# Gate and up sums of a feed-forward as seven block products in place of eight

## The chip, the cores and the metric

The kernel runs on one NeuronCore of a Trainium2 chip. What counts is its time on the device in microseconds (us), the median of several executions. A profile is one more execution, recorded by the hardware: for every engine, which instruction ran when. The engines are TensorE (PE; its weight loads are shown as PEld), VectorE (DVE), ScalarE (ACT), GpSimd (POOL) and SyncE (SP), which here starts the transfers from memory. SBUF is the working memory of 128 partitions, PSUM the eight banks into which TensorE sums.

## What is computed

A trunk of two decoder layers on 512 tokens of 1024 features: the first layer mixes the tokens by a convolution module, the second by differential attention. Behind each follow a SwiGLU feed-forward of 2816 hidden features and a gated per-layer input. The change concerns the two feed-forwards:

```python
def rms_norm(x, g):
    y = xf * lax.rsqrt(jnp.mean(xf * xf, axis=-1, keepdims=True) + EPS)
    return (y * g.astype(jnp.float32)).astype(x.dtype)

def swiglu(x, w_gate, w_up, w_down):
    return (jax.nn.silu(x @ w_gate) * (x @ w_up)) @ w_down

u = rms_norm(h, ffn_norm_g[i])
h = h + swiglu(u, ffn_w_gate[i], ffn_w_up[i], ffn_w_down[i])
```

All arrays are float32.

## The kernel before

**Tiling.** Everything is held transposed: a chunk is 128 features (partitions) by 512 tokens. `h[0]` to `h[7]` is the state. A product needs more precision than one pass of TensorE gives on operands of type fp32r, so every operand is split in a high part (`hi`, a cast on ScalarE) and a low part (`lo`, the rest, a subtraction on VectorE), and `mm3` (L161 to L165) sums three passes: low weight by high input, high by high, high by low. `weight` (L144 to L159) loads 128 output features by up to 1024 inputs (512 KB) to a raw tile and splits it: the cast is L156, the subtraction L158. A tag such as `wraw` or `whi` names a set of buffers, and the second number its count: two `wraw`, four `whi`, four `wlo`. The tags `A`, `B`, `C`, `D` name buffers that the stages use in turn.

**The norm.** `Norm.split` (L213) multiplies a chunk of `h` by the norm's gain and splits it; the factor of each token, which needs the sum of squares over all chunks, comes later: `columns`, `diagonal` and `rows` make of it a row `rb` that is the same on all partitions (the copy is L255). The sums are made of the inputs without that factor, and `rb` is multiplied in at the eviction.

**The feed-forward** (`ffn`, L641 to L671) goes through the 22 hidden chunks in three parts of 8, 8 and 6. For each chunk it makes the gate sum and the up sum, eight input chunks by three passes each, and then evicts them: VectorE multiplies by `rb` (L657, L659), ScalarE applies Silu (L658), VectorE multiplies gate and up (L660), and the hidden chunk is split to the tile `B{i}` (L662, L663). At the end of a part `linear` (L609) makes the down sums: for each of eight output chunks m the products with the part's hidden chunks, added to `h[m]` by L667. The first two output chunks are made together, the others one by one. The sums take four PSUM banks (`mm`) in turn. In the second feed-forward the first operands come out of attention, else it is the same.

**The order of the work.** The program's text gives each instruction a place, but a planner that follows a model of the engines' times sets the order in which each engine's queue holds them: what is ready early may come ahead of what stands earlier in the text, and a tile is given a buffer of its tag when one is free. On the chip each engine then takes its queue in order, and waits where an instruction's inputs or its buffer are not ready. The transfers of weights are all issued from SP's queue.

**Lines the change touches.** `mm3` (L161), `Norm.split` (L213), the split behind the convolution (L600), `linear` (L609), `ffn` (L641), `stage_o` (L907) with the same tiles as `Norm.split`, and the order of the weights in memory (`_layout`, L1053).

Of the kernel before, what the change touches and what calls it, by code (L numbers as in the profile page):

```python
# [77 lines left out]
LT = 2  # L78
LA = 4
PACK = True  # L80
E1 = True
GLO = 1
QKV = (("q", 0, (0, 0, 0, 0)), ("v", 0, (1, 1, 1, 2)), ("q", 1, (1, 1, 1, 2)), ("q", 2, (1, 1, 2, 1)), ("v", 1, (1, 1, 2, 2)), ("q", 3, (1, 1, 1, 1)))
# [5 lines left out]
def trunk(ctx, tc, xT, pT, wts, diag, dww, vec, rel, onehot, lamv, out):  # L89
# [68 lines left out]
                eng.tensor_tensor(lo[:, cut], raw[:, cut], f(hi[:, cut]), ALU.subtract)  # L158
        return hi, lo  # L159

    def mm3(acc, a, b, first, last):  # L161
        (ah, al), (bh, bl) = a, b
        T.matmul(acc, al, bh, start=first, stop=False)  # L163
        T.matmul(acc, ah, bh, start=False, stop=False)  # L164
        return T.matmul(acc, ah, bl, start=False, stop=last)  # L165

    def weight_in_h(i, c):

# [37 lines left out]
    class Norm:  # L206
# [388 lines left out]
    with tc.manual_schedule(engines={V.engine, A.engine}):  # L595
        for c in range(NC + 2):
            if c < NC:
                V.tensor_tensor(y[c], y[c], lrow, ALU.mult)
                A.activation(y[c], y[c], AF.Silu, scale=col("ln_g", c), bias=col("ln_b", c))
                z.append((sb([P, S], f"A{2 * c}", 1, F32R), sb([P, S], f"A{2 * c + 1}", 1, F32R)))  # L600
# [8 lines left out]
    def linear(n_in, src, consume, group0=1, before=None, after=None, split={}, home=None, given={}):  # L609
# [31 lines left out]
    def ffn(norm, after):  # L641
        rb = None
        for at, (f0, n) in enumerate(PARTS):
            hid = []
            for i in range(n):
                wg, wu = weight(), weight()
                pg, pu = mm(), mm()
                for k in range(NC):
                    mm3(pg, wpart(wg, k), norm.u[k], k == 0, k == NC - 1)
                if rb is None:  # L650
                    norm.diagonal()
                for k in range(NC):
                    mm3(pu, wpart(wu, k), norm.u[k], k == 0, k == NC - 1)
                if rb is None:
                    rb = norm.rows()
                tg, tu = big(), big()
                V.tensor_tensor(tg, pg, rb, ALU.mult)  # L657
                A.activation(tg, tg, AF.Silu)  # L658
                V.tensor_tensor(tu, pu, rb, ALU.mult)  # L659
                V.tensor_tensor(tu, tu, tg, ALU.mult)  # L660
                hl = sb([P, 2, S], f"B{i}", 1, F32R)
                A.copy(hl[:, 0], tu)  # L662
                V.tensor_tensor(hl[:, 1], tu, f(hl[:, 0]), ALU.subtract)  # L663
                hid.append((hl[:, 0], hl[:, 1]))

            def add(m, acc):
                V.tensor_tensor(h[m], acc, h[m], ALU.add)  # L667
                if at == len(PARTS) - 1:
                    after.chunk(m)

            linear(n, hid, add, 2)  # L671

    def ple(norm, pp, after, last_cuts=1):
        def sums(m, cuts=1):
# [22 lines left out]
        for m in range(2, NC):  # L697
            for part in sums(m, last_cuts if m == NC - 1 else 1):
                gate(*part)

    n2 = Norm("ple_g0")
    ffn(norm, n2)
    norm = Norm("attn_g")
    ple(n2, pp, lambda m, cut: norm.chunk(m))

# [201 lines left out]
    def stage_o(hd):  # L907
        t = tp()
        for i in range(4):
            T.transpose(t[:, i * P : (i + 1) * P], osb[hd][:, i * P : (i + 1) * P], ident)  # L910
        hi = sb([P, S], f"A{2 * hd}", 1, F32R)
        lo = sb([P, S], f"A{2 * hd + 1}", 1, F32R)
        split_scaled(t, gains[:, 1:2], hi, lo)
        ot[hd] = (hi, lo)

# [99 lines left out]

    order = {m: last_block for m in (2, 3, 4, 5)}
    linear(NC, ot, add_attn, 2, heads_until, step, split=order, given={0: w_o0, 1: w_o1})
    n2 = Norm("ple_g1")
    ffn(norm, n2)

    def store(m, cut):
        nc.sync.dma_start(out[m][:, cut], h[m][:, cut])
# [30 lines left out]
def _layout(a):  # L1053
# [12 lines left out]
    def ffn(i):  # L1066
        g, u = _stationary(a["ffn_w_gate"][i]), _stationary(a["ffn_w_up"][i])
        r = []
        for f0, n in PARTS:
            for c in range(f0, f0 + n):  # L1070
                r += [g[c], u[c]]
            r += list(pad(_stationary(a["ffn_w_down"][i][f0 * P : (f0 + n) * P])))
        return r

# [77 lines left out]
```

## Time and profile before

| | |
|---|---|
| time, median of three runs | 1274.49 us (1273.96 to 1274.73) |
| profiled execution | span 1273.4 us, its only time on the page |
| instructions | 15438 |
| HBM read and written | 128.84 MB and 6.31 MB |
| granted TensorE clock, mean | 0.999 |

The span goes from the first to the last instruction. A row of a group shows line, engine, operation and tiles, then count, busy time and mean duration of one in ns, then the idle time of the engine just before them and what ended it. A row of the timeline begins with the start and the duration in us; the bracket is idle time before it with what ended it. Matmuls are pipelined: a row's 0.39 us is longer than the step from one start to the next. A row of a stretch shows its bounds, its length and the busy time of PE, PEld, DVE, ACT and POOL with their counts, then the granted clock, the share of the DMA engines and GB/s.

### The profile page before, as it was taken

The page shows a single profiled execution, that of the slowest core. Times are in us where ns is not written, and L with a number is a line of the kernel's source. Part 1 is how long each engine was busy: PE and PEld are TensorE (multiplying, and loading weights), DVE is VectorE, ACT ScalarE, POOL GpSimd, SP SyncE. Part 2 cuts the span into 40 slices and gives each one's busy share as a digit, 9 for nine tenths or more (in the row PEclk, how much of TensorE's full clock was granted, in tenths as well). Part 3 has the DMA queues.
Part 4 walks back from the last instruction along what each step waited for, and adds up shares of the span by engine and source line. Part 5 has one row for each costly group of instructions (what it writes and reads, how often), then busy time and mean ns, then how long its engine had stood idle before and what let it go on. Part 6 is the DMA issues. An engine that isn't in the chain of part 4 may idle for free.

```text
span 1273.4 us, 15438 instructions
## 1 busy us (share of the span) xinstructions
PE 1261.1 (99%) x5928; PEld 1046.3 (82%) x5928; DVE 714.3 (56%) x1042; ACT 523.5 (41%) x876; POOL 251.8 (20%) x227
## 2 busy tenths in 40 slices
PE   8999999999999999999999999999999999999998
PEld 7888788888888888888888888888888888888887
DVE  6997866543344334456776876655443444334545
ACT  5652554322233213244666877644221232123332
POOL 2763432000000000042436635131000000000120
PEclk9999999999999999999999999999999999999999
DMA  7565223223232222233432320242222222222231
GB/s 261 171 217 192 75 73 110 99 100 94 88 99 100 99 99 93 65 127 136 136 114 78 99 100 24 71 130 97 100 96 90 96 99 100 99 93 90 85 114 66
DMA packets 49141, 136.15 MB, mean 107 GB/s; under 512 B 5635, under 2 KB 10243, under 8 KB 49068
## 3 DMA queue, kind: packets, MB, share of 16 engines
q1 hardware_dynamic: 46944, 131.74, 30.9%
q10 hardware_dynamic: 2124, 3.43, 0.9%
q8 instruction: 46, 0.75, 0.2%
q14 instruction: 27, 0.22, 0.1%
HBM read 128.84 MB, written 6.31 MB: 106 GB/s over the span
## 4 chain that ended last, share of the span: by engine, by line
PE 90%; DVE 3%; DMA 1%; issue 0%; SPq 0%; ACT 0%; POOL 0%; DVEq 0%
PE mm L163 28%; PE mm L164 28%; PE mm L165 28%; PE mm L880 1%; DVE sc L447 1%; PE sc L848 1%; PE sc L847 1%; PE tp L867 1%; PE sc L396 1%; PE mm L396 1%; PE tp L801 1%; PE mm L352 1%; PE tp L196 0%; DVE wlo L158 0%; DVE big L522 0%
## 5 line engine op out<-in xcount | busy, mean ns | idle before, releaser
L156 ACT CAST whi<-wraw 128x1024 fp32r<-128x1024 f32 (+2 forms) x209 | 213.1, 1026 | 555.5 <-PE mm L165 365.3
L163 PE MATMUL mm<-A,wlo 128*128 128x512 f32 (+1 forms) x1080 | 421.1, 390 | 2.2 <-ACT A L203 2.1
L164 PE MATMUL mm<-A,whi 128*128 128x512 f32 (+1 forms) x1080 | 418.5, 388 | 0.0
L165 PE MATMUL mm<-A,whi 128*128 128x512 f32 (+1 forms) x1080 | 416.5, 389 | 0.0
L158 DVE TENSOR_TENSOR wlo<-wraw,whi 128x1024 fp32r<-128x1024 f32 (+2 forms) x205 | 256.2, 1254 | 78.7 <-ACT whi L156 78.7
L163 PEld LDWEIGHTS mm<-A,wlo 128*128 128x128 f32 x1080 | 202.8, 188 | 45.5 <-ACT A L203 2.4
L164 PEld LDWEIGHTS mm<-A,whi 128*128 128x128 f32 x1080 | 202.8, 188 | 42.2 <-issue 1.0
L165 PEld LDWEIGHTS mm<-A,whi 128*128 128x128 f32 x1080 | 202.6, 188 | 41.9 <-issue 0.5
L227 POOL TENSOR_TENSOR acc<-acc,wk 128x512 f32<-128x512 f32 x35 | 57.9, 1654 | 773.1 <-issue 660.1
L163 PE MATMUL mm<-B,wlo 128*128 128x512 f32 x352 | 137.8, 391 | 0.0
L164 PE MATMUL mm<-B,whi 128*128 128x512 f32 x352 | 137.4, 390 | 0.0
L165 PE MATMUL mm<-B,whi 128*128 128x512 f32 x352 | 137.4, 390 | 0.0
L667 DVE TENSOR_TENSOR h<-mm,h 128x512 f32<-128x512 f32 x48 | 33.0, 691 | 123.0 <-PE mm L165 122.9
L659 DVE TENSOR_TENSOR big<-mm,rb 128x512 f32<-128x512 f32 x44 | 30.4, 691 | 126.4 <-PE mm L165 126.4
L657 DVE TENSOR_TENSOR big<-mm,rb 128x512 f32<-128x512 f32 x44 | 30.4, 691 | 99.5 <-PE mm L165 92.6
L165 PEld LDWEIGHTS mm<-B,whi 128*128 128x128 f32 x352 | 66.1, 188 | 14.5
L163 PEld LDWEIGHTS mm<-B,wlo 128*128 128x128 f32 x352 | 66.1, 188 | 14.3
L164 PEld LDWEIGHTS mm<-B,whi 128*128 128x128 f32 x352 | 66.1, 188 | 14.3
L163 PE MATMUL mm<-whi,A 128*128 128x512 f32 x192 | 76.5, 401 | 0.0
L165 PE MATMUL mm<-wlo,A 128*128 128x512 f32 x192 | 75.2, 398 | 0.0
L164 PE MATMUL mm<-whi,A 128*128 128x512 f32 x192 | 75.1, 393 | 0.0
L435 POOL TENSOR_TENSOR wk<-wk,C 128x512 f32<-128x512 f32 x35 | 53.6, 1532 | 14.6 <-ACT C L434 8.1
(227 smaller groups left out, 1377.6 us busy)
## 6 DMA issues: line engine op xcount, KB each, us to landing
wraw<-in_wts SPq DMA_DIRECT2D x193, 512.0 KB, 3.5
wraw<-in_wts SPq DMA_DIRECT2D x16, 384.0 KB, 2.9
D<-in_diag SPq DMA_DIRECT2D x22, 256.0 KB, 4.3
C<-in_diag SPq DMA_DIRECT2D x16, 256.0 KB, 4.6
h<-in_xT SPq DMA_DIRECT2D x8, 256.0 KB, 5.8
rest<-h SPq DMA_DIRECT2D x8, 256.0 KB, 2.8
bias<-scr ACTq DMA_DIRECT2D x8, 256.0 KB, 3.2
h<-rest SPq DMA_DIRECT2D x8, 256.0 KB, 2.7
```

The costliest lines, as they stand in the source:

```text
L156: A.copy(hi[:, cut], raw[:, cut])
L158: eng.tensor_tensor(lo[:, cut], raw[:, cut], f(hi[:, cut]), ALU.subtract)
L163: T.matmul(acc, al, bh, start=first, stop=False)
L164: T.matmul(acc, ah, bh, start=False, stop=False)
L165: return T.matmul(acc, ah, bl, start=False, stop=last)
L227: self.last = self.eng.tensor_tensor(self.acc, self.acc, sq, ALU.add)
L352: last_tap[0] = T.matmul(acc, dg[:, j % 4], ups[c][:, j : j + S], start=(j == 0), stop=(j == PE_TAPS[c] - 1))
L396: last_tap[0] = T.matmul(acc[:, g * P : (g + 1) * P], w, ups[c][:, g, LEAD - m : LEAD - m + P], start=(m == 0), stop=(m == LAGS - 1),)
L435: G.tensor_tensor(pacc, pacc, pr, ALU.add)
L657: V.tensor_tensor(tg, pg, rb, ALU.mult)
L659: V.tensor_tensor(tu, pu, rb, ALU.mult)
L667: V.tensor_tensor(h[m], acc, h[m], ALU.add)
```

## The change

The first four chunks of part 0 stay as they were. The other 18 chunks go in **units**: a unit makes two chunks of the gate (or two of the up) for all tokens. Its weights form a 2 x 2 matrix of blocks A11, A12, A21, A22 (rows: the two output chunks; columns: inputs 0 to 511 and 512 to 1023), the inputs a matrix B11, B12, B21, B22 (rows: the halves of the inputs; columns: the halves of the tokens, 256 each). The plain way is eight block products. Here there are seven, of sums S1 to S4 of weight blocks and T1 to T4 of input blocks (Strassen's scheme in Winograd's form); a block product is four input chunks by three passes by 256 tokens.

- `operands` runs once in a feed-forward, behind the first plain chunk. It makes `u` = h x gain x `rb` (VectorE), so that the factor of the norm is in the operands and not in the eviction, the four T sums (GpSimd), and splits all. They stay in tiles that the stage has free (`spare0`, `spare1`).
- `Unit.load` fetches the two weight tiles of a unit, by turns to `wraw` and to the tiles A0 and A1. `Unit.prep` makes the four S sums on GpSimd and splits A11 with A12, S1 with S2, S4 with A22 (128x1024 each, to `whi` and `wlo`) and S3.
- `Unit.p(i)` is product i, with its part of the eviction. Products that share a sum add into the same half of a PSUM bank. What remains is added on VectorE from PSUM to a tile in SBUF.
- `run` orders the products: P1, P2, then P4 of the unit before, P6, P3 of the unit before, P5, P7; between them the steps of `prep` for the next unit.
- `linear` gets a hook: at output chunk 6 the first unit of the next part is loaded and prepared.
- High and low parts of a normed chunk are halves of one tile now.

```diff
@@ def split
-            hi = sb([P, S], f"A{2 * c}", 1, F32R)
-            lo = sb([P, S], f"A{2 * c + 1}", 1, F32R)
+            hi, lo = both(sb([P, 2, S], f"A{c}", 1, F32R))
@@ def linear
+            if m in at:
+                at[m]()
@@
+    def operands(norm, rb, spare):
+        ub = [sb([P, 2, S], f"B{4 + j}", 1) for j in range(4)]
+        u = [ub[c // 2][:, c % 2] for c in range(NC)]
...
+        for k in range(4):
+            for c in (k, k + 4):
+                V.scalar_tensor_tensor(u[c], h[c], col(norm.g, c), rb, ALU.mult, ALU.mult)
+            (u11, u12), (u21, u22) = ((u[c][:, :HT], u[c][:, HT:]) for c in (k, k + 4))
+            hi, lo = low[k]
+            A.copy(hi, u11)
+            V.tensor_tensor(lo, u11, f(hi), ALU.subtract)
+            ops["B11"][k] = hi, lo
+            hi, lo = uppers(k)
+            A.copy(hi, u[k + 4])
+            V.tensor_tensor(lo, u[k + 4], f(hi), ALU.subtract)
...
+            t = sb([P, 4, HT], f"B{2 + k % 2}", 1)
+            G.tensor_tensor(t[:, 0], u12, u11, ALU.subtract)
+            G.tensor_tensor(t[:, 1], u22, t[:, 0], ALU.subtract)
+            G.tensor_tensor(t[:, 2], u22, u12, ALU.subtract)
+            G.tensor_tensor(t[:, 3], u21, t[:, 1], ALU.subtract)
+            hi, lo = tops(k)
+            A.copy(hi, t)
+            V.tensor_tensor(lo, t, f(hi), ALU.subtract)
...
+        def two(self, src, a, b):
+            hi, lo = sb([P, 2, S], "whi", 4, F32R), sb([P, 2, S], "wlo", 4, F32R)
+            A.copy(hi, src)
+            V.tensor_tensor(lo, src, f(hi), ALU.subtract)
...
+        def prep(self, step):
+            (r0, r1), s, s3 = self.raw, self.sums, self.s3
+            if step == 0:
+                self.two(r0, "A11", "A12")
+            elif step == 1:
+                G.tensor_tensor(s[:, 0], r1[:, 0], r1[:, 1], ALU.add)
+                G.tensor_tensor(s[:, 1], s[:, 0], r0[:, 0], ALU.subtract)
+            elif step == 2:
+                self.two(s, "S1", "S2")
+            elif step == 3:
+                G.tensor_tensor(s3, r0[:, 0], r1[:, 0], ALU.subtract)
+                G.tensor_tensor(r1[:, 0], r0[:, 1], s[:, 1], ALU.subtract)
+            elif step == 4:
...
+                self.w["S3"] = hi, lo
+            else:
+                self.two(r1, "S4", "A22")
...
+        def p(self, i):
+            if i == 1:
+                self.a, self.c = mm(), mm()
+            a, lo, hi = self.a[:, :HT], self.c[:, :HT], self.c[:, HT:]
+            acc, w, b, first = {
+                1: (a, "A11", "B11", True), 2: (hi, "A12", "B21", True), 6: (a, "S2", "T2", False),
+                5: (lo, "S1", "T1", True), 7: (a, "S3", "T3", False), 4: (a, "A22", "T4", False),
+                3: (lo, "S4", "B22", False),
+            }[i]
+            self.product(acc, w, b, first)
...
+        def run(us):
+            for n, x in enumerate(us):
+                last = us[n - 1] if n else None
+                nxt = us[n + 1] if n + 1 < len(us) else None
+                x.start()
+                if nxt:
+                    nxt.load()
+                x.p(1)
+                if nxt:
+                    nxt.prep(0)
+                x.p(2)
+                if nxt:
+                    nxt.prep(1)
+                if last:
+                    last.p(4)
+                x.p(6)
...
+            us[-1].p(4)
+            us[-1].p(3)
@@ def ffn
-            hid = []
-            for i in range(n):
+            for i in range(PLAIN if at == 0 else 0):
...
+                if i == 0:
+                    ops = operands(norm, rb, spare)
+            if at == 0:
+                us = units(at, PLAIN, n, hid)
+                begin(us)
+            run(us)
...
+                hooks[6] = lambda: begin(us2)
-            linear(n, hid, add, 2)
+            linear(n, hid, add, 2, at=hooks)
```

A gate unit ends with Silu on its four quarters. An up unit ends with the multiplication by the gate's chunks and the split of two hidden chunks.

More of the change, by code (lines that the diff above doesn't have):

```diff
@@ L80 @@
 PACK = True
+PLAIN = 4
+HT = S // 2
 E1 = True
@@ new lines, in trunk, with start, ready @@
+    class Gate(Unit):
+        def start(self):
+            self.out = big(), big()
+        def ready(self, j, k):
+            cut = slice(k * HT, (k + 1) * HT)
+            src = self.a[:, :HT] if (j, k) == (1, 0) else self.out[j][:, cut]
+            A.activation(self.out[j][:, cut], src, AF.Silu)
+    class Up(Unit):
+        def start(self):
+            self.out = wk(), wk()
+            self.done = [0, 0]
+        def ready(self, j, k):
+            o, g = self.out[j], self.gate.out[j]
+            cut = slice(k * HT, (k + 1) * HT)
+            if j == 1:
+                V.tensor_tensor(o[:, cut], self.a[:, :HT] if k == 0 else o[:, cut], g[:, cut], ALU.mult)
+            self.done[j] += 1
+            if self.done[j] < 2:
+                return
+            if j == 0:
+                V.tensor_tensor(o, o, g, ALU.mult)
+            hid = both(sb([P, 2, S], f"B{self.at + j}", 1, F32R))
+            A.copy(hid[0], o)
+            V.tensor_tensor(hid[1], o, f(hid[0]), ALU.subtract)
+            self.hid[self.at + j] = hid
@@ new lines, in ffn, with units, begin @@
+    def ffn(norm, after, spare):
+        rb = None
+        ops = None
+        early = []
+        def units(at, f0, n, hid):
+            us = []
+            for i in range(f0, n, 2):
+                k = len(us)
+                raws = "wraw" if k % 2 == (0 if at == 0 else 1) else "A"
+                g = Gate(k, at == 0 and k == 0, raws)
+                u = Up(k + 1, False, "A" if raws == "wraw" else "wraw")
+                u.gate, u.at, u.hid = g, i, hid
+                us += [g, u]
+            for x in us:
+                x.b = ops
+            return us
+        def begin(us):
+            us[0].load()
+            for step in range(6):
+                us[0].prep(step)
+        def run(us):
[14 more added lines that the diff above has]
+                x.p(6)
+                if nxt:
+                    nxt.prep(2)
+                if last:
+                    last.p(3)
+                x.p(5)
+                if nxt:
+                    nxt.prep(3)
+                    nxt.prep(4)
+                x.p(7)
+                if nxt:
+                    nxt.prep(5)
+            us[-1].p(4)
+            us[-1].p(3)
+        for at, (f0, n) in enumerate(PARTS):
+            if at == 0:
+                hid = [None] * n
+            else:
+                hid = hid2
+            for i in range(PLAIN if at == 0 else 0):
@@ L699, in ple, with spare0, uppers @@
                 gate(*part)
+    def spare0():
+        pairs = {1: ("C5", 2), 2: ("C5", 2), 3: ("C4", 2)}
+        def uppers(k):
+            if k == 0:
+                return sb([P, S], "wth", 2, F32R), sb([P, S], "wtl", 2, F32R)
+            return both(sb([P, 2, S], *pairs[k], F32R))
+        return tops(lambda k: f"C{k}"), uppers, lowers
     n2 = Norm("ple_g0")
-    ffn(norm, n2)
+    ffn(norm, n2, spare0)
     norm = Norm("attn_g")
```

107 lines of the change are left out of this document (95 added, 12 removed).

## The prediction, made before the changed kernel was run

> **What bounds the kernel now.** I read the page's busy table and its chain first, then the groups of instructions, then the timeline of the feed-forward stage by engine.
>
> ```profile
> PE 1261.1 (99%) x5928; PEld 1046.3 (82%) x5928; DVE 714.3 (56%) x1042; ACT 523.5 (41%) x876; POOL 251.8 (20%) x227
> PE 90%; DVE 3%; DMA 1%; issue 0%; SPq 0%; ACT 0%; POOL 0%; DVEq 0%
> ```
>
> TensorE is busy 99% of the span, and 90% of the chain that ended last is TensorE. So the kernel is as long as its matmuls, and two questions decide: how much TensorE time the change removes, and whether the other engines keep TensorE fed in the new order. The window in the middle of part 0 and the evictions of chunks 1 to 3 give the rate.
>
> ```profile
> 226.40:248.15 21.75, 21.75 (x97) 18.02 (x96) 10.07 (x13) 6.52 (x8) 0.00 (x0) 1.00 0.29 100
> 226.39 0.69 DVE L659 TENSOR_TENSOR big<-mm,rb 128x512 f32<-128x512 f32 x1 [0.55 <-PE mm L165]
> 231.83 0.69 DVE L657 TENSOR_TENSOR big<-mm,rb 128x512 f32<-128x512 f32 x1 [2.29 <-PE mm L165]
> 248.15 0.69 DVE L659 TENSOR_TENSOR big<-mm,rb 128x512 f32<-128x512 f32 x1 [3.09 <-PE mm L165]
> ```
>
> The first row is a stretch: TensorE is busy for all 21.75 us, VectorE (third figure) for 10.07, ScalarE 6.52, GpSimd not at all, granted clock 1.00. The evictions come 5.44 us apart, one product of 24 matmuls of 512 columns: 0.2267 us each. Two chunks of gate (or of up), 48 matmuls, cost 10.88 us, a pair of units (two gate chunks and two up chunks) 21.76.
>
> **TensorE's side of the change.** The halves need matmuls of 256 columns. The trace has 48 of them, the two halves of the last product (L163 to L165); these are the first and the last.
>
> ```profile
> 1262.64 0.28 PE L163 MATMUL mm<-A,wlo 128*128 128x256 f32 x1
> 1268.28 0.28 PE L165 MATMUL mm<-A,whi 128*128 128x256 f32 x1
> ```
>
> 47 steps in 5.64 us: 0.120 us each, each with a weight load of its own. A unit of the change has 7 products x 4 input blocks x 3 = 84 matmuls, so 84 x 0.120 = 10.08 us in place of 10.88. There are 18 chunks x 2 (gate, up) / 2 = 18 units in each feed-forward, 36 in all: 36 x 0.80 = **28.8 us less**. That is 2.3%, not the eighth that seven for eight suggests, since a half-width matmul costs 53% of a whole one.
>
> The Trainium skill, "TensorE: Matmul & The Clock Gate", section "Back-to-back issue gap", gives a warm gap of N / 2.4 + 2.5 ns, about 109 ns and 216 ns here. By it a unit would go from 10.4 to 9.2 us and the gain be some 43 us. The rows above are slower in both shapes and decide.
>
> The matmuls that read a hidden chunk are a little slower: the evictions of the down sums lie further apart.
>
> ```profile
> 450.24 0.69 DVE L667 TENSOR_TENSOR h<-mm,h 128x512 f32<-128x512 f32 x1 [3.20 <-PE mm L165]
> 455.75 0.69 DVE L667 TENSOR_TENSOR h<-mm,h 128x512 f32<-128x512 f32 x1 [3.20 <-PE mm L165]
> ```
>
> 5.51 us against 5.44, 1.3% more for the same 24 matmuls. What causes it the trace does not say; the new operands lie in other buffers, so I bound it by 0 and 1.3% of 3024 x 0.120 = 363 us, 0 to 5 us, and take **+3**.
>
> **What the other engines get.** These rows give the prices (durations are minimum/median/maximum).
>
> ```profile
> L158 DVE TENSOR_TENSOR wlo<-wraw,whi x205: 693/1224/2655, 4.1 to 1248.4; 128x1024 fp32r<-128x1024 f32 x93, 128x768 fp32r<-128x768 f32 x8, 128x512 fp32r<-128x512 f32 x2
> L688 DVE TENSOR_TENSOR h<-h,big x17: 424/687/1664, 587.7 to 1270.0; 128x512 f32<-128x512 f32 x15, 128x256 f32<-128x256 f32 x2
> L435 POOL TENSOR_TENSOR wk<-wk,C x35: 1267/1295/2297, 37.1 to 143.0; 128x512 f32<-128x512 f32 x35
> 840.55 2.35 DVE L158 TENSOR_TENSOR wlo<-wraw,whi 128x1024 fp32r<-128x1024 f32 x2
> L156 ACT CAST whi<-wraw 128x1024 fp32r<-128x1024 f32 x189 | 197.4, 1051 | 506.1 <-PE mm L165 339.3 <-issue 138.5 <-DMA wraw<-in_wts 27.4
> L662 ACT CAST B<-big 128x512 fp32r<-128x512 f32 x44 | 27.5, 625 | 19.7 <-DVE big L660 19.6
> ```
>
> VectorE: 1.22 us for 1024 elements, 0.69 for 512, 0.42 for 256; back to back some 0.09 less (two of 1.22 in 2.35). GpSimd: 1.28 for 512. A pair of units needs on VectorE six low parts of 1024, five operations of 512 (two S3, one multiply, two hidden low parts) and eight of 256: 7.3 + 3.5 + 3.4 = 14.2 us. GpSimd gets eight sums, 8 x 1.28 = 10.2. ScalarE gets six casts of 1.05, four of 0.62 and some ten of 256 (0.41, by the step from 1.05 to 0.62): 12.9 us. Each alone fits under TensorE's 20.16 us. But VectorE and GpSimd do not run side by side on such operands:
>
> ```profile
> 655.63 2.41 POOL L158 TENSOR_TENSOR wlo<-wraw,whi 128x1024 fp32r<-128x1024 f32 x1 [5.43 <-ACT whi L156]
> 656.90 2.22 DVE L158 TENSOR_TENSOR wlo<-wraw,whi 128x1024 fp32r<-128x1024 f32 x1 [0.22 <-ACT whi L156]
> ```
>
> GpSimd's operation ends at 658.04. VectorE's, begun at 656.90, takes 2.22 us instead of 1.22 and ends at 659.12, 1.08 us after GpSimd's end: it did nothing until then. So one waits for the other's whole instruction. The Trainium skill, "SBUF — State Buffer", section "Who interferes with whom", says this as a rule: a VectorE instruction with two SBUF inputs and a GpSimd instruction that reads SBUF exclude each other, and the second blocks. By that rule, the trace agrees; without it the next two terms would shrink to about 6 us together.
>
> In turns, a pair costs VectorE and GpSimd 24.4 us less the starts that overlap (19 x 0.09 and 8 x 0.13, the part of GpSimd's 1.28 that isn't data: 2.41 - 1.28 = 1.13 for 512 elements), 21.7 us. The seven operations that read PSUM (2.4 us) may lie beside a GpSimd one, so the bounds are 19.3 and 21.7 against TensorE's 20.16. **This change takes VectorE from half busy to the edge.**
>
> Steady units: a lead hides a shortfall. With four whi buffers and three used by each unit, a unit's first weights can be made from the end of the second product of the unit before, 7.2 us ahead of use, for 1.05 + 1.22 us of work: 4.8 us of lead, refilled during each down sum, where VectorE is busy for 15 of 43 us:
>
> ```profile
> 425.00:468.00 43.00, 43.00 (x189) 35.16 (x189) 15.05 (x18) 8.32 (x8) 0.00 (x0) 1.00 0.29 98
> ```
>
> Parts 1 and 2 have 4 and 3 pairs; at worst 4 x 1.5 - 4.8 = 1.2 us are left, plus gaps of engines that run in order. I take 0.18 us for each of 28 units, **+5** (0 to 14).
>
> Start of a feed-forward: here there is no lead.
>
> ```profile
> 220.22 0.59 ACT L255 COPY rb<-tp 128x512 f32<-128x512 f32 x1 [4.07 <-PE tp L280]
> 220.84 0.69 DVE L657 TENSOR_TENSOR big<-mm,rb 128x512 f32<-128x512 f32 x1 [3.43 <-ACT rb L255]
> 226.43 1.05 ACT L156 CAST whi<-wraw 128x1024 fp32r<-128x1024 f32 x1 [1.32 <-PE mm L165]
> ```
>
> The norm's row is there at 220.8 and chunk 3 ends at 248.15: 27.3 us. The new scaled operands need, for each of four k, two products h x g x rb (0.66 each, back to back), low parts of 256, 512 and 1024 (0.34, 0.60, 1.13) and four GpSimd sums of 256 (0.57 of data each): 5.7 us in turns, 22.7 for all. With them go chunks 0 to 2 (3.6 us of SBUF and 4.2 of PSUM operations, half of these hidden), the last two weights' low parts (2.3) and unit 0's first (1.1). P1 needs about 28 of this, P6 (all T2, S2) some 35 us, and without a stall P6 starts 2.9 + 27.3 us after 220.8. So P6 comes some 4 us late. Unit 1 then has 8.6 us until its own P6 for 10 us of work, 1.5 late, and the rest of part 0 runs even, another 1.5. **+7 for each feed-forward, +14** (bounds 0, if the PSUM operations all hide and the hidden chunks' low parts are put off; 34, if nothing overlaps and each engine's order leaves gaps).
>
> Passing from a down sum to the next part: the hook at m = 6 gives three of four whi buffers to the next unit, so weights 6 and 7 wait for product 5 and 6. In program order each costs a cast and a low part with nothing before them, 1.05 + 1.22 + 0.3 = 2.6 us, 2 x 4 passages, 21 us. But the order on TensorE is a planner's, not the program's:
>
> ```profile
> 215.10 1.05 ACT L156 CAST whi<-wraw 128x1024 fp32r<-128x1024 f32 x1 [2.16 <-PE mm L165]
> 219.16 1.02 PE L280 MATMUL tp<-wk,ones 128*128 128x512 f32 x2
> ```
>
> The up product of chunk 0 ended at 215.1 and the spread that follows it in the program came at 219.16, with chunk 1's gate ahead of it. In the same way P1 and P2 of the next unit (2.9 us) can fill the wait for weight 6, and P2 frees a buffer for weight 7. I take **+2** (0 to 21).
>
> At nothing: the norm's and attention's halves in one tile (same instructions, covered by TensorE; a wait for both halves costs at most one 0.7 us step once), and the DMAs: SP issues two of 512 KB for a unit where there were two, at the same 100 GB/s; those for A0 and A1 wait for VectorE's last read of the unit before last, 10 us early.
>
> **Sum**: -28.8 + 3 + 5 + 14 + 2 = -4.8 us on the profiled execution, whose only time is its span of 1273.4; the runs' median of 1274.5 is 1.1 above. 1274.5 - 4.8 = **1269.7 us**, 0.4% faster; own range 1260 to 1277.
>
> **Rivals.** (1) VectorE and GpSimd in turns become the bound of all units. With 2% of gaps a pair takes 22.1 us (21.7 and 2%), against 21.76 before: 18 x 0.34 = 6, and the scaled operands delay each start by 4.5: 1274.5 + 6 + 9 = **1290**. It decides from about 21.3 us for a pair; the blocked pair of rows speaks for it, the lead and the refill against it. (2) All is hidden: VectorE's PSUM work lies beside GpSimd's and the planner finds the room: 1274.5 - 28.8 + 3 + 1 = **1250**. Against it stands the start. (3) TensorE keeps the program's order at the four passages, 19 more than the forecast: **1289**. (4) The halves don't run at half price: at a weight load's 0.19 us a unit would take 15.8 us; the 48 matmuls above exclude it.
>
> **Chances.** Forecast 0.43 (0.35 faster, 0.06 within 0.2%, 0.02 slower), rival 1 0.37 (0.04 within), rival 2 0.09, rival 3 0.08, worse starts 0.03: faster 0.44, same 0.10, slower 0.46. 0.2% (2.5 us) is about what a measurement of this kernel can tell from no change. The range leaves out part of rival 2 and the far end of rival 1: 1252 to 1294.
>
> **What would show it.** 256-column steps of 0.120 to 0.122; GpSimd's 512 sums at 1.3 to 2.2 us and VectorE's low parts above 1.22 where they meet; TensorE's idle time ahead of L163, ended by VectorE's low parts, mostly in the first 20 us behind the plain chunks; almost none in part 2. Idle time spread evenly over all units, with VectorE over 95%, would be rival 1; idle time before the last two down sums, rival 3.

## The result, and the profile after

The changed kernel takes **1311.6 us** (median of four runs, 1309.75 to 1314.42) against 1274.4 us (1273.96 to 1274.73): ratio 1.0293, 95% interval 1.0279 to 1.0308. It is 2.9% slower; the prediction was 1269.7, with a range up to 1294. The profiled execution took 1314.42 us, its span is 1312.6, its mean granted clock 0.978 (0.999 before). Two of the profiled executions told of below were disturbed (3916.6 us at a clock of 1.000, 1363.0 us at 0.848), so those two kernels have a second run, whose profile is read.

The page's busy table and its chain by engine:

```profile
PE 1254.8 (96%) x7224; PEld 1099.4 (84%) x7224; DVE 890.8 (68%) x1208; ACT 634.5 (48%) x1116; POOL 537.4 (41%) x403
PE 77%; DVE 8%; issue 3%; POOL 3%; DMA 2%; ACT 1%; SPq 0%; POOLq 0%; DVEq 0%; ACTq 0%
```

The table looks harmless: VectorE rose to 68%, far from full. The second line is the one to read. TensorE's share of the chain fell from 90 to 77%; VectorE's rose to 8, GpSimd's to 3. The groups of TensorE say where it stood still (the last field is its idle time ahead of the group, and what ended it; before, it was 0.0 ahead of the down sums, `mm<-B`, and 2.2 in all ahead of the largest group, `mm<-A,wlo`):

```profile
L165 PE MATMUL mm<-C,wlo 128*128 128x256 f32 x540 | 154.3, 286 | 18.7 <-ACT big L754 18.7
L165 PE MATMUL mm<-B,wlo 128*128 128x512 f32 x352 | 143.4, 407 | 21.8 <-DVE wlo L160 21.8
L165 PE MATMUL mm<-wth,wlo 128*128 128x256 f32 (+1 forms) x152 | 46.1, 303 | 6.8 <-DVE wlo L712 6.1 <-DVE big L762 0.7
```

18.7 + 21.8 + 6.8 = **47.3 us of idle time**. L754 is the eviction of P1, L160 the low part of a plain weight (here: for the down sums), L712 that of a unit's weights. In time the waits lie at few places. The first unit of the first feed-forward:

```profile
249.01 0.28 PE L166 MATMUL mm<-wth,whi 128*128 128x256 f32 x1
...
250.21 0.28 PE L167 MATMUL mm<-C,whi 128*128 128x256 f32 x1
259.59 0.58 PE L165 MATMUL mm<-C,wlo 128*128 128x256 f32 x1 [9.10 <-ACT big L754]
...
262.10 0.41 PE L167 MATMUL mm<-C,whi 128*128 128x256 f32 x1
265.19 0.58 PE L165 MATMUL mm<-wth,wlo 128*128 128x256 f32 x1 [2.67 <-DVE wlo L712]
...
270.48 0.29 PE L165 MATMUL mm<-wth,wlo 128*128 128x256 f32 x1
```

The first two rows are ten steps apart, 0.120 us each. P6 comes 9.1 us late, and the next unit's P1 another 2.7: the start of a feed-forward. And the passage from part 0's down sums to part 1 (PE, ACT, DVE and POOL rows in order of time):

```profile
331.34 1.05 ACT L711 CAST whi<-A 128x1024 fp32r<-128x1024 f32 x1 [4.46 <-PE mm L167]
...
336.37 0.39 PE L167 MATMUL mm<-B,whi 128*128 128x512 f32 x1
336.79 1.04 ACT L158 CAST whi<-wraw 128x1024 fp32r<-128x1024 f32 x1 [4.40 <-PE mm L167]
337.87 1.86 DVE L160 TENSOR_TENSOR wlo<-wraw,whi 128x1024 fp32r<-128x1024 f32 x1 [0.38 <-ACT whi L158]
338.60 2.25 POOL L726 TENSOR_TENSOR A<-A,A 128x512 f32<-128x512 f32 x1
339.78 0.80 PE L165 MATMUL mm<-B,wlo 128*128 128x512 f32 x1 [3.03 <-DVE wlo L160]
345.50 0.44 PE L166 MATMUL mm<-B,whi 128*128 128x512 f32 x1
348.28 1.04 ACT L158 CAST whi<-wraw 128x1024 fp32r<-128x1024 f32 x1 [10.44 <-PE mm L167]
350.63 0.50 PE L165 MATMUL mm<-B,wlo 128*128 128x512 f32 x1 [2.40 <-DVE wlo L160]
```

The next unit's cast (331.34) has taken the last `whi` buffer. The cast of weight 6 begins when TensorE's last matmul of product 5 is through, its low part follows, and only then does product 6 start: 3.0 us with nothing on TensorE between. The same again for weight 7, 2.4 us. From 339.78 to 345.50 there are 13 steps in 5.72 us, 0.44 each instead of 0.227. The stretches show why (the granted clock is the third figure from the end):

```profile
262.00:266.00 4.00, 1.32 (x6) 1.03 (x6) 4.00 (x3) 1.84 (x3) 3.92 (x3) 0.50 0.00 0
341.00:346.00 5.00, 5.00 (x14) 3.85 (x13) 0.00 (x0) 0.00 (x0) 2.37 (x2) 0.54 0.26 95
351.00:356.00 5.00, 5.00 (x23) 4.10 (x22) 0.00 (x0) 0.00 (x0) 0.65 (x1) 1.00 0.39 108
360.00:437.00 77.00, 76.24 (x629) 75.66 (x629) 64.43 (x67) 42.37 (x73) 43.57 (x25) 1.00 0.34 103
```

Behind the start's waits and behind the one of 3.03 us the granted clock is 0.50 for some microseconds, and TensorE is "busy" all the while; behind the one of 2.40 us (third row) it is 1.00. The last row is the steady part 1: 0.76 us idle in 77, although VectorE is busy for 64.43 us of them.

**The account.** -28.8 (units) + 47.3 (idle) + the rest: the span grew by 1312.6 - 1273.4 = 39.2, so the rest is 39.2 + 28.8 - 47.3 = **20.7 us, nearly all of it time at half clock**. The stretches give that part by itself: for every microsecond from 200 to 1240, the busy time of TensorE times what the granted clock lacks of 1 sums to **19.0 us**, 8.2 at the two starts and 10.8 at the passages (0.0 in the kernel before). It can also be counted in steps at one start: eleven steps of P6 take 2.51 us (259.59 to 262.10) instead of 1.32, and the 24 that follow, P1 of the next unit and P7 of the first, 5.29 (265.19 to 270.48) instead of 2.88, **3.6 us** together.

### The profile page after: what moved, and what is told of

Its sections match the earlier page's. It is cut to its first block, busy times and chain, and to the rows that moved or that the text cites. A ratio compares the mean times of both kernels' runs of the same rounds, so it can differ in the third digit from the quotient of the medians.

```text
span 1312.6 us, 18775 instructions
## 1 busy us (share of the span) xinstructions
PE 1254.8 (96%) x7224; PEld 1099.4 (84%) x7224; DVE 890.8 (68%) x1208; ACT 634.5 (48%) x1116; POOL 537.4 (41%) x403
## 4 chain that ended last, share of the span: by engine, by line
PE 77%; DVE 8%; issue 3%; POOL 3%; DMA 2%; ACT 1%; SPq 0%; POOLq 0%; DVEq 0%; ACTq 0%
PE mm L165 24%; PE mm L166 23%; PE mm L167 23%; DVE wlo L160 2%; DVE wlo L712 1%; PE mm L1121 1%; DMA wraw<-in_wts 1%; DVE sc L448 1%; PE sc L1089 1%; PE sc L1088 1%; PE tp L1108 1%; ACT whi L158 1%; PE sc L397 1%; PE mm L397 1%; DVE B L663 1%
## 5 line engine op out<-in xcount | busy, mean ns | idle before, releaser
L160 DVE TENSOR_TENSOR wlo<-wraw,whi 128x1024 fp32r<-128x1024 f32 (+2 forms) x133 | 175.7, 1327 | 63.8 <-ACT whi L158 63.6
L165 PE MATMUL mm<-A,wlo 128*128 128x512 f32 (+1 forms) x504 | 197.2, 392 | 0.1
L166 PE MATMUL mm<-A,whi 128*128 128x512 f32 (+1 forms) x504 | 194.6, 387 | 0.0
L167 PE MATMUL mm<-A,whi 128*128 128x512 f32 (+1 forms) x504 | 192.5, 389 | 0.0
L165 PE MATMUL mm<-C,wlo 128*128 128x256 f32 x540 | 154.3, 286 | 18.7 <-ACT big L754 18.7
L165 PE MATMUL mm<-B,wlo 128*128 128x512 f32 x352 | 143.4, 407 | 21.8 <-DVE wlo L160 21.8
L166 PE MATMUL mm<-C,whi 128*128 128x256 f32 x540 | 153.9, 285 | 0.0
L167 PE MATMUL mm<-C,whi 128*128 128x256 f32 x540 | 153.8, 285 | 0.0
L712 DVE TENSOR_TENSOR wlo<-A,whi 128x1024 fp32r<-128x1024 f32 x70 | 113.1, 1622 | 16.5 <-ACT whi L711 16.3
L165 PEld LDWEIGHTS mm<-C,wlo 128*128 128x128 f32 x540 | 104.5, 194 | 19.6 <-ACT big L754 19.3
L165 PEld LDWEIGHTS mm<-A,wlo 128*128 128x128 f32 x504 | 94.8, 188 | 20.7 <-issue 1.4
L166 PEld LDWEIGHTS mm<-A,whi 128*128 128x128 f32 x504 | 94.9, 188 | 19.5 <-issue 1.0
L167 PEld LDWEIGHTS mm<-A,whi 128*128 128x128 f32 x504 | 94.5, 188 | 19.5 <-issue 0.5
L166 PEld LDWEIGHTS mm<-C,whi 128*128 128x128 f32 x540 | 104.7, 194 | 0.2
L167 PEld LDWEIGHTS mm<-C,whi 128*128 128x128 f32 x540 | 104.7, 194 | 0.0
```

The lines of the kernel that those rows point to most:

```text
L165: T.matmul(acc, al, bh, start=first, stop=False, **kw)
L166: T.matmul(acc, ah, bh, start=False, stop=False, **kw)
L167: return T.matmul(acc, ah, bl, start=False, stop=last, **kw)
L712: V.tensor_tensor(lo, src, f(hi), ALU.subtract)
```

## The experiments

**Theory 1**: two separate places cost the gain, the start of each feed-forward (VectorE, GpSimd and ScalarE prepare the operands in a chain that three plain chunks don't cover) and the four passages (the next unit's preparation holds three of four weight buffers); at both, the granted clock halves behind most of the waits. **Theory 1a** says of the start that it is mostly GpSimd's turns that hold VectorE up; **1b**, that it is the order of the queues and the two buffers of the T sums. The rivals are the prediction's first (all units are slowed by VectorE and GpSimd) and a common cost that comes back elsewhere.

**1. Buffers of its own for weight 6** (`e1_aside`), two tiles that are idle there:

```diff
-                else weight(n_in * P, after=split.get(m + i, (None, None)), home=home if m + i == 2 else None)
+                else weight(n_in * P, after=split.get(m + i, (None, None)), home=home if m + i == 2 else None,
+                            parts=("A3", "A5") if at and m + i == 6 else None)
```

> The changed kernel (1311.6 us) with one edit: the split weights of down sum 6 go to two tiles of the A group that are free in the down sums, not to the four whi buffers, so that weight 7 can have the buffer that down sum 5 gives back. Theory 1 (the four passages lose time because three of four whi buffers are taken by the next unit, and TensorE keeps the program's order): the waits ahead of down sums 6 and 7 (3.2 and 2.6 us beyond a step, four times, 23 us) go, and with them about half of the matmuls at half clock (some 10 us): 1276 to 1282 us. Rival (the low parts are late there because VectorE and GpSimd take turns, or the transfer is late): the waits stay, 1306 to 1312 us.

Measured: **1277.4 us** (ratio to before 1.0020, 1.0011 to 1.0030), 34.2 us less than the changed kernel. One pair of buffers at the passages is worth 34 us, although the idle time there is 21.8: the half clock went with it.

**2. The same kernel again, for its profile** (`e8_aside_again`):

> The first run's kernel once more, for its profile: weight 6 has two buffers of its own at the passages. Theory 1: no wait of over 1 us ahead of the last two down sums of parts 1 and 2, the clock at 1.00 there, the waits at the two starts as in the changed kernel (9.4 and 3.1), 1276 to 1279 us.

Measured: 1277.8 us, span 1275.1. The group that stood idle for 21.8 us:

```profile
L165 PE MATMUL mm<-B,wlo 128*128 128x512 f32 x320 | 125.5, 392 | 0.0
```

The waits are gone, and a matmul of the group (without the 32 of product 6, which now reads other tiles) lasts 392 ns instead of 407: that is the half clock, of which the stretches now show 6.3 us, all at the starts. The waits at the starts are as they were (18.2 us of idle time in the group behind L755, the changed kernel's L754).

**3. No buffer more, only another order** (`e6_begin_last`): the next part's unit begins behind the last down sum.

```diff
-                hooks[6] = lambda: begin(us2)
-            linear(n, hid, add, 2, at=hooks)
+            linear(n, hid, add, 2)
             if at < len(PARTS) - 1:
+                begin(us2)
```

> The same number of buffers, only another order: the next part's first unit is loaded and cast behind the last down sum in the program (so behind the casts of weights 6 and 7), not ahead of chunk 6. Theory 1 (at the passages the three casts of the next unit hold the weight buffers that weights 6 and 7 need): the eight waits ahead of the last two down sums are gone and the half clock behind them; the next unit's first casts then take the buffers of weights 4 to 6, free before its product needs them: 1276 to 1286 us. Rival (the passage simply holds more casts, low parts and GpSimd sums than the engines can do in its time): the waits come back at P1, P2 or P6 of the next unit, of like size, and 1300 to 1312 us.

Measured: **1277.4 us** (1.0025, 1.0016 to 1.0034): all of it again. ScalarE's casts in this kernel:

```profile
323.82 1.05 ACT L158 CAST whi<-wraw 128x1024 fp32r<-128x1024 f32 x1 [4.08 <-DMA wraw<-in_wts]
325.76 1.05 ACT L158 CAST whi<-wraw 128x1024 fp32r<-128x1024 f32 x1 [0.89 <-PE mm L167]
331.27 1.05 ACT L711 CAST whi<-A 128x1024 fp32r<-128x1024 f32 x1 [4.45 <-PE mm L167]
```

The last plain weights are cast at 323.8 and 325.8 (336.8 and 348.3 in the changed kernel), and the unit's casts stand behind them. The rival (too much work for the passage) falls: it is the same work. So the cause at the passages is who gets the buffers, and the order in the text decides it.

**4. Six plain chunks instead of four** (`e2_plain6`): two chunks more cover the preparation, and 32 units are left of 36.

```diff
-PLAIN = 4
+PLAIN = 6
```

> The changed kernel with six plain chunks in place of four, so 16 chunks in units: the scaled operands have 10.9 us more until their first use and each feed-forward gives up two units, 1.6 us. Theory 1 (the start loses time because the operands and the first unit's weights are not ready, 12.2 us of waits in each feed-forward, and 3.6 us at half clock behind them): nearly all of it goes, 1311.6 - 2 x (12 + 3) + 3 = 1281 to 1288 us. Rival (the waits come with the first units, whose eviction stands behind casts in ScalarE's queue, and move along with them): 1308 to 1316 us.

Measured: **1289.0 us** (1.0118, 1.0101 to 1.0135), 22.6 less than the changed kernel and 1 above the range. Four units less cost 3.2 us, so the cover is worth 25.8. The weight loads that waited (the PEld rows) at the first start:

```profile
272.70 0.19 PEld L165 LDWEIGHTS mm<-C,wlo 128*128 128x128 f32 x1 [0.72 <-ACT big L754]
279.46 0.19 PEld L165 LDWEIGHTS mm<-C,B 128*128 128x128 f32 x1 [1.79 <-ACT big L759]
```

Of 9.3 and 3.0 us of such waits are left 0.7 and 1.8, and no half clock at the starts. The waits at the passages are as in the changed kernel.

**5. Both** (`e7_both`): experiments 1 and 4 together.

> Two changes of the earlier runs together: buffers of its own for weight 6 at the passages (the first run, -34.2 us) and six plain chunks instead of four (the second, -22.6 us). Theory 1 (starts and passages are separate places, and a unit is worth 0.80 us where nothing waits): 1311.6 - 34.2 - 22.6 = 1254.8, so 1251 to 1259 us, faster than the kernel before by 1.2 to 1.8%. Rival (they share a cost, the half clock or the engines' load): 1262 to 1275.

Measured: **1255.2 us** (0.9847, 0.9833 to 0.9860). 1311.6 - 34.2 - 22.6 = 1254.8: the two places simply add, and a kernel with Strassen's units is 1.5% faster than before once they are out of the way. The clock is 1.00.

**6. The T sums on VectorE** (`e3_tsum_v`), so that GpSimd doesn't take turns with it on the operands:

```diff
-            G.tensor_tensor(t[:, 0], u12, u11, ALU.subtract)
+            V.tensor_tensor(t[:, 0], u12, u11, ALU.subtract)
```

and the same for the other three.

> The changed kernel with the sixteen T sums of the operands on VectorE in place of GpSimd. Theory 1a (VectorE and GpSimd take turns on these operands, and that makes them late): VectorE has 16 x 0.34 = 5.4 us more, but no turns to wait for; the last low part of T is there about 10 us earlier, the wait of 9.4 us ahead of P6 shrinks to 0 to 3 us in each feed-forward: 1285 to 1297 us. Rival 1b (the order of the queues and the two buffers of T make the gaps, GpSimd 6.7 us idle for a buffer and VectorE 6.3 us idle for a cast): the buffers and the order are as before, the wait stays or grows by VectorE's 5 us: 1308 to 1322 us.

Measured: **1305.1 us** (1.0241, 1.0224 to 1.0258), between the two ranges. The eight scaled operands, here and then in the changed kernel:

```profile
L663 DVE SCALAR_TENSOR_TENSOR B<-h,vec,rb 128x512 f32<-128x512 f32 x8 | 5.4, 746 | 0.0
```

```profile
L663 DVE SCALAR_TENSOR_TENSOR B<-h,vec,rb 128x512 f32<-128x512 f32 x8 | 8.3, 1106 | 0.0
```

The turns are real: 2.9 us in this group alone. But the waits at the start only move:

```profile
254.11 0.29 PEld L165 LDWEIGHTS mm<-C,wlo 128*128 128x128 f32 x1 [3.42 <-ACT whi L711]
259.34 0.29 PEld L165 LDWEIGHTS mm<-wth,wlo 128*128 128x128 f32 x1 [3.88 <-DVE wlo L712]
...
276.62 0.19 PEld L165 LDWEIGHTS mm<-wth,wlo 128*128 128x128 f32 x1 [1.59 <-DVE big L762]
```

8.9 us in these three rows instead of some 12. The time lies between the ranges of 1a and 1b, so neither has it alone.

**7. The first unit's weight sums on VectorE** (`e10_first_v`; the base is experiment 3):

```diff
+            E = V if self.first else G
-                G.tensor_tensor(s[:, 0], r1[:, 0], r1[:, 1], ALU.add)
+                E.tensor_tensor(s[:, 0], r1[:, 0], r1[:, 1], ALU.add)
```

and the same for the other three.

> The sixth kernel (begun last, four plain chunks, 1277.4 us), with the four sums of each feed-forward's first unit (S1, S2, S3, S4: 512 columns each) on VectorE instead of GpSimd; the inputs' sums T1 to T4 stay on GpSimd. Theory 1 (the start is late by the chain between the engines: the casts of the weight sums wait for GpSimd, which takes them behind the inputs' sums, and P1's eviction and the low parts wait behind those casts): P6's wait of 9.4 us falls to 2 to 5 and P1's or P5's after it is at most as long as now: 1262 to 1272 us. Rival (VectorE has simply too much to do before P6, and now 4 x 0.7 us more): the waits stay at 12 us in sum or grow, 1275 to 1283.

Measured: **1271.1 us** (0.9967, 0.9953 to 0.9981), 6.3 less than its base, in the range. The same kernel for its profile (`e11_first_again`):

> The tenth kernel once more, for its profile. Theory 1 (the chain of engines): P6 of the first unit waits 2 to 5 us instead of 9.4, the product after it no longer than 5, clock at half for a few us behind the longer one; 1269 to 1273 us. Rival: the waits still come to 12 us in sum and the gain of 6 us is somewhere else.

Measured: 1270.0 us (0.9963). The time is as expected and the reason given for it is not:

```profile
261.10 0.29 PEld L165 LDWEIGHTS mm<-C,wlo 128*128 128x128 f32 x1 [9.90 <-ACT whi L711]
```

P6 still waits 9.9 us; what went is the second wait. VectorE's queue in this kernel:

```profile
246.65 0.69 DVE L723 TENSOR_TENSOR B<-B,wraw 128x512 f32<-128x512 f32 x1
251.14 1.48 DVE L681 TENSOR_TENSOR C<-B,C 128x1024 fp32r<-128x1024 f32 x1 [3.80 <-ACT C L680]
...
259.77 1.21 DVE L712 TENSOR_TENSOR wlo<-B,whi 128x1024 fp32r<-128x1024 f32 x1
```

The sums S1 and S2 are ready at 247.3, but their low part stands in the queue behind low parts of T, which wait for GpSimd by way of ScalarE.

**8. Both kinds of sums on VectorE** (`e12_all_v`; experiments 6 and 7 on the base of 3):

> The tenth kernel (begun last, four plain chunks, the first unit's weight sums on VectorE) with the inputs' sums T1 to T4 on VectorE too, so that GpSimd has only the second unit's weight sums at a start. Without any wait four plain chunks would give 1274.4 - 28.8 + 1 = 1246.6 us, so the start still costs 1271 - 1247 = 24 us in the tenth kernel. Theory 1 (a chain between engines, of which VectorE's own work is now the longest piece): half of that is left, 1254 to 1264 us, slower than with six plain chunks. Rival (VectorE becomes the bound of the start: 16 sums of 0.4 and 4 of 0.7 us more): 1266 to 1280.

Measured: **1268.8 us** (0.9952, 0.9936 to 0.9969), above theory 1's range and inside the rival's, 8.6 less than the base. Most of what is left at the start is one wait:

```profile
255.19 0.29 PEld L165 LDWEIGHTS mm<-C,wlo 128*128 128x128 f32 x1 [4.96 <-ACT whi L711]
```

The first unit is still 5 us late. ScalarE's cast of S1 and S2 (first row), their low part on VectorE (last row), and some of what lies between:

```profile
246.90 1.05 ACT L711 CAST whi<-B 128x1024 fp32r<-128x1024 f32 x1 [2.23 <-DVE B L723]
249.35 1.51 DVE L677 TENSOR_TENSOR B<-B,B 128x256 f32<-128x256 f32 x1
250.54 1.44 POOL L723 TENSOR_TENSOR A<-A,A 128x512 f32<-128x512 f32 x1
250.78 1.75 DVE L728 TENSOR_TENSOR wraw<-wraw,B 128x512 f32<-128x512 f32 x1
253.86 1.21 DVE L712 TENSOR_TENSOR wlo<-B,whi 128x1024 fp32r<-128x1024 f32 x1
```

VectorE has no gap from 220.3 us on, so its own load counts. But GpSimd isn't out of the way: it makes the second unit's weight sums from 247.85 to 253.66, and the four operations of VectorE beside them take 5.95 us together, where four of their sizes take 2.0 just before. And the low part that P6 waits for stands behind these four, 5.9 us after its cast ended. How much of the 5 us is load, how much turns and how much order was not tested. The time fell by little although the waits shrank: TensorE's idle time is 7.0 us less than in `e11_first_again` (25.2 instead of 32.2), but its busy time 4.7 more, and the half clock by the stretches 8.1 us instead of 4.0. The clock was low for 20.5 us in both; behind the shorter waits more matmuls fell into that time.

**9. The best of all** (`e9_three`): experiment 3's order, six plain chunks, T sums on VectorE.

> Three changes together: the next part's first unit begun behind the last down sum (as in the sixth run, no buffer more), six plain chunks, and the sums T1 to T4 of the inputs on VectorE. Theory 1: the passages are free as in the seventh run, and of the two places where that run's TensorE still waits at a start (0.6 and 1.9 us) the second, behind the sums of S3 and S4 on GpSimd, goes, since GpSimd has no T sums ahead of them: 1249 to 1255 us. Rival (16 sums of 256 columns more on VectorE, some 0.4 us each, stand ahead of the plain chunks' products and of the low parts, and TensorE waits for those): 1257 to 1265.

Measured: **1251.3 us** (0.9820, 0.9806 to 0.9835), the fastest of the study, 23.1 us below the kernel before. Its page:

```profile
PE 1236.7 (99%) x7080; PEld 1080.2 (86%) x7080; DVE 883.8 (71%) x1226; ACT 624.2 (50%) x1092; POOL 475.9 (38%) x355
```

VectorE has nearly the busy time of the changed kernel (883.8 against 890.8) and TensorE is busy 99% of the span. 32 units save 25.6, which would be 1248.8: 2.5 us are left to all starts, passages and steady units.

**10. The clock by itself** (`e4_fill`): useless products of 128 columns keep TensorE busy where it waits; they take the place of the waits and gain nothing of them.

```diff
+                r = x.p(2)
+                if x.first:
+                    idle(80, r)
...
+        def idle(n, behind):
+            t = tp()
+            with tc.issue_after(behind.ins):
+                for _ in range(n):
+                    T.matmul(t[:, 0:P], ident, ones, start=True, stop=True)
```

and 26 of them ahead of the down sums 6 and 7.

> The changed kernel with 80 matmuls of no use (ident by ones, 128x128) between P2 and P6 of the first unit of each feed-forward and 26 ahead of down sums 6 and 7 of parts 0 and 1, into an unused PSUM bank: they fill the waits, so that TensorE does not stand still. Theory 1c (behind each wait TensorE runs at half clock for some us, 18 us in all): the granted clock stays at 1.00 in the feed-forwards and the time falls by 10 to 18 us, 1294 to 1302 us, with the waits' ends where they were. Rival (the half clock costs nothing there, since the waits that follow take it up): 1308 to 1314 us.

Measured: **1329.4 us** (1.0436, 1.0421 to 1.0452), a miss for both theories. The clock was 1.00 and the waits were gone, but a product of these f32 operands takes 222 ns, two records of 111 each, so the fills lasted twice as long as the waits. They ran again with half the number (`e5_fill2`):

> The useless products of the fourth run again, but as many as the waits are long: one took 222 ns there (160 records of 111.2 ns in the first place, 52 of 110.0 in the others), so that its places filled 17.8 us where the wait was 9.4 and 5.7 us where it was 2.8 to 3.5. Now 42 products (9.3 us) behind P2 of each feed-forward's first unit and 13 (2.9 us) ahead of the down sums of chunks 6 and 7. They take the place of the waits and gain nothing of them; outside them the output's sums are unchanged. Theory 1 (about 18 us of the loss are TensorE at half its granted clock behind the waits): 1291 to 1297 us at a clock of at least 0.99. Rival (the clock's records are a by-product and the time behind the waits is lost to something else): 1308 to 1314.

Measured: **1308.1 us** (1.0262, 1.0248 to 1.0276), 3.5 below the changed kernel: by its number the rival's, so the expectation of theory 1 is missed. The trace tells the two places apart. At the passages the fills did what was meant; two stretches of this kernel:

```profile
339.00:341.00 2.00, 2.00 (x15) 1.81 (x14) 0.96 (x1) 0.00 (x0) 2.00 (x1) 1.00 0.05 10
341.00:346.00 5.00, 5.00 (x24) 4.11 (x24) 0.13 (x1) 0.13 (x1) 2.64 (x3) 1.00 0.30 102
```

The clock stays at 1.00, with 24 matmuls where the changed kernel had 14. From the first to the last addition to `h`, where the passages lie, the two feed-forwards take 265.2 and 264.8 us instead of 271.1 and 268.7: 9.8 less, though 8 fills of 2.9 us stand where 21.8 us were idle. So the half clock behind the passages' waits is worth some 11 us, as the stretches say (10.8); experiment 1 agrees, 34.2 - 21.8 = 12. At the starts the time did not fall, because the order behind the fill became another, and a new wait came after it:

```profile
266.65 0.29 PEld L165 LDWEIGHTS mm<-C,wlo 128*128 128x128 f32 x1 [5.70 <-DVE big L759]
```

A fill holds the clock, but the operands come no earlier for it: fill and wait are 9.3 + 5.5 us at a start, where 11.8 were idle. Over the whole kernel TensorE's busy time without the fills (188 of 0.222 us) is 1239.8 us instead of 1254.8, 15.0 less, and the half clock by the stretches 3.7 us instead of 19.0, 15.3 less. So the expectation failed mostly by the longer waits at the starts; the half clock has nearly the size that theory 1 gave it. Its part is shown at the passages by two experiments; at the starts it rests on the counted steps and the stretches.

## Why the prediction was wrong

The sum was -28.8 + 3 + 5 + 14 + 2 = -4.8 us. Step by step:

- **Units, -28.8: right.** The 256-column steps are 0.120 us (249.01 to 250.21), and in experiment 9, where nearly nothing waits, 32 units should give 25.6 and 23.1 arrived.
- **Slower operand steps, +3, and steady units, +5: too much.** The steps are at 0.120, and in the stretch of part 1 TensorE is idle for 0.76 us in 77, so of the 8 us perhaps 2 or 3 came. Rival 1, which had a chance of 0.37, is refuted: VectorE and GpSimd do block one another, and in the steady units TensorE does not wait for it. Its own mark, idle time spread over all units, is absent. (In the working of the turns, the part of GpSimd's 1.28 us that isn't data is 1.28 - 1.13 = 0.15, not 0.13, which makes a pair 21.5 us instead of 21.7; nothing hangs on it.)
- **Passages, +2: the step that failed most.** It said that the planner would put P1 and P2 of the next unit ahead of product 6, as it had put chunk 1's gate ahead of the norm's spread. It did not: nothing stands between 336.37 and 339.78. Why the planner kept the order here isn't shown. The failure is in the kind of evidence. A row that shows a planner's choice at one place was taken as a rule for another. Rival 3 had the mechanism with its place and its price (2.6 us a wait, 21 in all; 21.8 of idle time measured), at a chance of 0.08. Taking the cause away gave 34.2 us, in two different ways.
- **Start, +14: too small, by two things.** Some 12 us idle at the first start and some 3.6 of half clock, against 7. The working let VectorE and GpSimd alternate without gaps. In the trace both stand idle in that very stretch:

```profile
238.84 2.26 POOL L675 TENSOR_TENSOR B<-B 128x256 f32<-128x256 f32 x1 [6.65 <-DVE C L681]
...
251.00 1.04 ACT L711 CAST whi<-B 128x1024 fp32r<-128x1024 f32 x1 [4.44 <-POOL B L722]
252.08 1.33 DVE L712 TENSOR_TENSOR wlo<-B,whi 128x1024 fp32r<-128x1024 f32 x1 [6.25 <-ACT whi L711]
...
259.17 0.36 ACT L754 COPY big<-mm 128x256 f32<-128x256 f32 x1
```

  GpSimd waits 6.65 us for a low part, since the T sums have two buffers; then ScalarE and VectorE wait 4.4 and 6.3 us for GpSimd's S2; and the eviction of P1 (259.17), ready since P1, stands behind the casts in ScalarE's queue. So P6 came 9 us late instead of 4. The engines' sums of work bound this only from below; the chain is longer. How much of it is buffers, how much queue order and how much load the runs don't separate to the end: experiments 6 to 8 took away 3 us per start each, 4 together, and the cover of two chunks nearly all. More T buffers weren't tried.
- **The half clock, not in the sum at all: 19 us by the stretches, 20.7 as the rest of the account.** Every wait was priced as its idle time. The kernel before never showed a wait of TensorE long enough for the clock to fall in the stages that the change touches (its clock is 1.00 in every microsecond from 200 to 1240), and the price of the matmuls behind a wait was taken from rows at clock 1.00.

So the sum with measured terms is -28.8 + 47.3 (idle) + 19.0 (half clock) = +37.5, and the span grew by 39.2; the 1.7 left are of the size of what experiment 9 leaves to all else, 2.5. The range ended at 1294 because it held each rival alone and priced none with a half clock. The starts at twice their size (12 + 3.6, twice: 31) and the passages with their half clock (34 by experiment 1) are 1274.5 - 28.8 + 31 + 34 = 1311.

Of the marks that the prediction named, the steps of 0.120 and GpSimd's sums at up to 2.25 us where the engines meet came true, and the idle time ahead of the last two down sums, the mark of rival 3, decided between the cases.

## What to carry to other kernels

When TensorE is 99% busy, price a wait that a change adds at its idle time and add something for the matmuls behind it at half clock: here nothing behind waits of up to 1.8 us, 1.7 us or nothing behind 2.4, mostly 1.5 to 3.1 behind 3.0, and 4.1 at a start with 11.8 us of waits. Where a stage hands its buffers to the next one, see who gets the last of them: the same work begun a few lines later in the text was worth 34 us here. And a chain of engines at a start is not bounded by the sum of their work; look for two engines that idle in the same stretch, and for cover that is cheap (two plain chunks more cost 1.6 us in each feed-forward and hid nearly 13).

## What the runs showed of the hardware

The granted clock halves behind short waits, and the length of the wait alone doesn't decide it. Behind 3.03 us without a matmul the steps were at half clock for 5.7 us (339.78 to 345.50); behind 2.40 us at 350.63 they were not (clock 1.00 in the stretch from 351 to 356); behind another 2.40 us in the same profile they were:

```profile
484.88 0.50 PE L165 MATMUL mm<-B,wlo 128*128 128x512 f32 x1 [2.40 <-DVE wlo L160]
484.00:489.00 5.00, 4.12 (x11) 3.26 (x12) 0.82 (x1) 0.00 (x0) 0.51 (x1) 0.66 0.34 105
```

Over the passages of the changed kernel and of experiments 4 and 6, the clock fell behind 10 of 12 waits of about 3.0 us (2.9 to 3.1) and behind 6 of 12 of 2.4 us. The two waits of 0.7 and 1.8 us in experiment 4 show no half clock by their stretch (1.00 from 247 to 303). The time at half clock, on the other hand, has a fixed grain. Counted from the stretches of 1 us it is 3.4, 6.8 or 17.1 us at a place of the changed kernel, and in sum 58.0 us there, 27.3 in experiment 2, 23.9 in experiment 4, 20.5 in experiment 8: 17, 8, 7 and 6 times 3.41. The Trainium skill, "TensorE: Matmul & The Clock Gate", section "Part 1: The HAM clock gate", states an idle window of about 3.4 us that halves the clock, and about as long a stretch of work that restores it. The trace agrees with the length of 3.4 us; as to the wait, it differs, since waits of 3.0 and 2.4 us were enough here. Fills with useless products kept the clock at 1.00, so it is the lack of matmuls that lowers it.

A matmul of 128 columns on f32 operands takes 222 ns, where one of 256 columns on the split operands takes 120. The row of the source line in `e5_fill2` shows 376 records for 188 instructions:

```profile
L862 PE MATMUL tp<-ones,ident x376: 272/275/275, 249.7 to 1156.0; 128*128 128x128 f32 x188
```
